# Splitting the wide products of stick-breaking attention, moving the small products of a head, and shifting two operands by 128 bytes

## The chip, the cores and the metric

The kernel runs on one core of one Trainium2 chip. The metric is the device time of one execution in microseconds (us). TensorE (PE) multiplies; VectorE (DVE) and ScalarE (ACT) prepare its operands and take its results away; SyncE (SP) issues the weight transfers; GpSimd (POOL) only fills constants.

## What is computed

A two-layer trunk over 272 positions (16 learned ones ahead of 256 given) of width 2048, in float32. Layer 0 is a Mamba-2 mixer and a gated feed-forward net. From its result one key and one value projection is made. Layer 1 is stick-breaking attention with its own query projection, and a second gated net. The part that the change touches, per head of width 128 and 16 heads:

```
q = (u @ w_q) ; z = q k^T * 128**-0.5
before = kpos < qpos
log_keep = where(before, log_sigmoid(-z), 0)
tail = reverse_cumsum(log_keep) - log_keep
att  = where(before, exp(log_sigmoid(z) + tail), 0)
o    = att @ v ; out = o @ w_o
```

## The kernel before

**A projection** (`project`, lines 140 to 174) makes one tile of 128 output columns for all positions. Its weights come in two halves of 8 blocks of 128 by 128. ACT rounds a half to the type fp32r (line 128, tile `hi`), DVE takes the rest (line 129, tile `lo`), and `mac` makes three matmuls for each block: high weights by low activations (line 142), high by high (143), low by high (144). So a tile is 16 blocks by 3 = 48 matmuls, 272 columns wide where all positions are needed (activations `u0`, `u1`, `y`, `hid`, `ukv`) and 256 wide for the 256 given positions (`uq` for queries, `ob` for the output projection, `u2` for the last gate and up products). There are five `hi` and four `lo` buffers, so ACT and DVE may work that far ahead of PE. `project_block` works on four tiles at a time, half by half, and calls `pump` after each half, which lets waiting side work go on.

**Attention.** The loop over 16 heads m makes the key tile (272 wide), the value tile (272) and the query tile (256); between value and query `others(m)` lets three older heads go on by one stage each. `attend` is a generator with three stages. Stage 1 (head m-1): the scores `psc`, in plain fp32, for queries 0 to 127 against 144 keys (line 685) and queries 128 to 255 against 272 keys (line 686); then mask, two sigmoids, a scan. Stage 2 (head m-2): PE transposes of values (`pt`, line 706) and weights (`pb`, line 710), copied to `vb` and `ab`. Stage 3 (head m-3): `po`, values by weights, in plain fp32, 256 wide (line 725) and 128 wide (line 726). A plain fp32 matmul shows as two records each of line 685, 686, 725 and 726; a transpose shows as one. Every fourth head has two more transposes (lines 713, 714) and a further product (line 728). "Small products" is what follows for this cluster. For the last head the value tile comes after the query, and the last stages of the last heads run between halves of the output projection's first block.

**The last feed-forward net** uses `u2`, and for its down projection a scheme with fewer products, all of whose matmuls are 256 wide and come from line 886 (`three`): stationary tile `sa`, moving tiles `hi`, `lo` and `lq`.

**Addresses.** SBUF tiles are laid out by the pools in the order written. All buffers of `hi` and `lo` start 96 bytes past a multiple of 256, and their blocks are 512 bytes apart. `pair` puts `pad` float32 elements ahead of an activation tile. In the program before, `uq`, `ob` and `u2` start 32 bytes past a multiple of 256, that is, 192 bytes past a multiple of 256 from their weights. `sa` starts at 96, so the moving `hi` and `lo` of line 886 also stand at 192 from it, and `lq` too. `beat` (lines 147 to 150) and `short` put a few 128-wide matmuls with no use for the result ahead of some streams.

Of the kernel before, what the change touches and what calls it, by code (L numbers as in the profile page):

```python
# [6 lines left out]
F32 = mybir.dt.float32  # L7
F32R = mybir.dt.float32r
AF = mybir.ActivationFunctionType
ALU = mybir.AluOpType  # L10
# [3 lines left out]
P = 128  # L14
D = 2048
KD = D // P
SEQ = 256
META = 16
T = SEQ + META
# [8 lines left out]
CONV = 4  # L28
# [5 lines left out]
OQ = 128  # L34
# [6 lines left out]
PAD = {"u": 0, "uq": 64, "y": 0, "ob": 0, "hid": 0, "sa": 16}  # L41
# [16 lines left out]
def trunk(tc, a, out):  # L58
    nc = tc.nc
    V, S, PE = nc.vector, nc.scalar, nc.tensor  # L60
    pin = tc.keep_in_program_order

    with tc.tile_pool(name="const", bufs=1) as cp, \
# [7 lines left out]
        upool = uctx.enter_context(tc.tile_pool(name="up", bufs=1, side="right"))  # L71
# [4 lines left out]

        for k, c in list(PIECES)[:2]:
            nc.scalar.dma_start(h[:, k:k + c, :], a["hT"][:, k:k + c, :])
        cw = upool.tile([P, CONV + 1, 48], F32, name="cw")
        gd = upool.tile([P, 2, 32], F32, name="gd")  # L80
        hd = upool.tile([NH, 2], F32, name="hd")

# [9 lines left out]
        nc.gpsimd.memset(ident, 0.0)  # L92
        nc.gpsimd.affine_select(out=ident, in_=ident, compare_op=ALU.not_equal, fill=1.0,
                                base=0, pattern=[[-1, P]], channel_multiplier=1)
        causal = upool.tile([P, T - OQ], F32, name="causal")
        nc.gpsimd.memset(causal, 1.0)
        nc.gpsimd.affine_select(out=causal, in_=causal, compare_op=ALU.is_ge, fill=0.0,
                                base=0, pattern=[[1, T - OQ]], channel_multiplier=-1)
        sel = upool.tile([P, P], F32, name="sel")
        nc.gpsimd.memset(sel, 1.0)  # L100
        nc.gpsimd.affine_select(out=sel, in_=sel, compare_op=ALU.is_ge, fill=0.0,
                                base=-(P - 1), pattern=[[0, P]], channel_multiplier=1)
# [3 lines left out]
        def nm(s):  # L106
            uid[0] += 1
            return f"{s}_{uid[0]}"
# [25 lines left out]
        def pair(pool, K, n, pad, step, tail=0, **kw):  # L134
            t = pool.tile([P, pad + 2 * K * step + tail], F32R, **kw)
            t = t[:, pad:pad + 2 * K * step].rearrange("p (s k t) -> p s k t", s=2, t=step)
            return [t[:, i, :, :n] for i in range(2)]
# [46 lines left out]
        def times(dst, ps, r):  # L184
            V.tensor_tensor(out=dst, in0=ps[:, :r.shape[-1]], in1=r, op=ALU.mult)
# [48 lines left out]
        u = pair(upool, KD, T, PAD["u"], TP, 24, tag="u", name="u0")  # L234
# [48 lines left out]
        with tc.tile_pool(name="ssd0", bufs=1) as q0, \  # L283
# [25 lines left out]
            with tc.tile_pool(name="dtp", bufs=1) as dq:  # L309

                psd = ptp.tile([P, 512], F32, tag="pt", name=nm("pt"))[:, :T]
                last = piece_w(*PIECES[-1])
                parts = [load(a["w_dt"], k0, LC, NH)[:, :, :NH] for k0 in range(0, KD, LC)]
                for i, w in enumerate(parts):
                    V.tensor_tensor(out=w, in0=w, op=ALU.mult,
                                    in1=gam[:, 0, i * LC:(i + 1) * LC].unsqueeze(2).to_broadcast([P, LC, NH]))
                for j in range(LC):
                    for i, w in enumerate(parts):
                        pin(PE.matmul(psd[i * NH:(i + 1) * NH], w[:, j, :], h[:, i * LC + j, :],  # L319
                                      start=j == 0, stop=j == LC - 1))  # L320
# [10 lines left out]
                v = dq.tile([NH, T], F32, name="v")  # L331
# [37 lines left out]
                pt = ptp.tile([P, 512], F32, tag="pt", name=nm("pt"))  # L369
# [221 lines left out]
            u = pair(upool, KD, T, PAD["u"], TP, 24, tag="u", name="u1")  # L591
# [46 lines left out]
        vpool = vctx.enter_context(tc.tile_pool(name="vp", bufs=1))  # L638
        with tc.tile_pool(name="att1", bufs=1) as b1p, \
                tc.tile_pool(name="att2", bufs=2) as b2p, \  # L640
                tc.tile_pool(name="psa", bufs=3, space=PSUM) as pap:
            uq = pair(vpool, KD, SEQ, PAD["uq"], SEQ, tag="v", name="uq")
            for k in range(KD):
                split_scaled(uq, k, h[:, k, META:], gam[:, 1, k:k + 1])
            ob = pair(b1p, KD, SEQ, PAD["ob"], SEQ, name="ob")
            L0, L1 = META + 128, T
            W = L0 + L1
# [28 lines left out]
            def flat(t):  # L676
                return t.rearrange("p h b k -> p (h b k)")

            def attend(m, kT, qT, vT, vs, ss, pk):
                i = m % SET
                S.copy(vs[:, i], vT.rearrange("p (b k) -> p b k", k=P)[:, 1:, :META])
                psc = pap.tile([P, 512], F32, tag="at", name=nm("psc"))
                PE.matmul(psc[:, :L0], qT[:, 0:128], kT[:, :L0], start=True, stop=True)  # L685
                PE.matmul(psc[:, L0:W], qT[:, 128:256], kT, start=True, stop=True)  # L686
                sc = b2p.tile([P, 2, T], F32, tag="sc", name=nm("sc"))
                ends = sc[:, :, P:L0]
                sc = sc.rearrange("p b k -> p (b k)")[:, :W]
                V.tensor_tensor(out=sc, in0=psc[:, :W], in1=mask, op=ALU.add)  # L690
                kp = b2p.tile([P, W], F32, tag="kp", name=nm("kp"))
                S.activation(kp, sc, AF.Sigmoid, scale=-SCALE)
                S.activation(sc, sc, AF.Sigmoid, scale=SCALE)

                tl = b2p.tile([P, 2, T], F32, tag="tl", name=nm("tl"), bufs=1)
                tails = tl[:, :, P:L0 - 1]
                tl = tl.rearrange("p b k -> p (b k)")
                n = W - 1
                V.tensor_tensor_scan(tl[:, n - 1::-1], kp[:, n:0:-1], reset[:, n - 1::-1],
                                     1.0, ALU.mult, ALU.max)  # L700
                V.tensor_tensor(out=ss[:, i, :, :META - 1], in0=ends[:, :, :META - 1], in1=tails, op=ALU.mult)
                V.tensor_tensor(out=sc[:, :n], in0=sc[:, :n], in1=tl[:, :n], op=ALU.mult)
                yield
                pt = prp.tile([P, 512], F32, tag="pr", name=nm("pt"))
                for b in range(2):
                    pin(PE.transpose(pt[:, b * P:(b + 1) * P], vT[:, b * P:(b + 1) * P], ident))
                vb = b2p.tile([P, 2 * P], F32, tag="vb", name=nm("vb"))
                pb = pap.tile([P, 512], F32, tag="at", name=nm("pb"))
                for b, c in enumerate((0, L0, L0 + P)):
                    pin(PE.transpose(pb[:, b * P:(b + 1) * P], sc[:, c:c + P], ident))  # L710
                ab = b2p.tile([P, 3 * P], F32, tag="ab", name=nm("ab"))
                if i == SET - 1:
                    pin(PE.transpose(pt[:, 256:384], flat(vs), ident))
                    pin(PE.transpose(pt[:, 384:512], flat(ss), ident))
                S.copy(ab, pb[:, :384])
                S.copy(vb, pt[:, :256])
                if i == SET - 1:
                    vsT = b1p.tile([P, P], F32, tag="vsT", name=nm("vsT"))
                    S.copy(vsT, pt[:, 256:384])
                    bd = b1p.tile([P, 2 * SET, META], F32, tag="bd", name=nm("bd"))  # L720
                    V.tensor_tensor(out=bd, in0=pt[:, 384 + E0:512].unsqueeze(1).to_broadcast([P, 2 * SET, META]),
                                    in1=own, op=ALU.mult)
                yield
                po = pap.tile([P, 512], F32, tag="at", name=nm("po"))
                PE.matmul(po[:, :SEQ], vb[:, :P], ab[:, 0:SEQ], start=True, stop=False)  # L725
                PE.matmul(po[:, P:SEQ], vb[:, P:], ab[:, SEQ:], start=False, stop=True)
                if i == SET - 1:
                    PE.matmul(po[:, SEQ:SEQ + P], vsT, bd.rearrange("p g q -> p (g q)"), start=True, stop=True)
                S.copy(ob[0][:, m, :], po[:, :SEQ])
                V.tensor_copy(pk[:, i], po[:, :SEQ].rearrange("p (b k) -> p b k", b=2)[:, :, E0:])  # L730
                V.tensor_tensor(out=ob[1][:, m, :], in0=po[:, :SEQ], in1=ob[0][:, m, :].bitcast(F32),
                                op=ALU.subtract)
                if i == SET - 1:
                    V.tensor_tensor(out=flat(pk), in0=flat(pk), in1=po[:, SEQ:SEQ + P], op=ALU.add)
                    oh, ol = [o[:, m - i:m + 1, :].rearrange("p h (b k) -> p h b k", b=2)[:, :, :, E0:] for o in ob]
                    S.copy(oh, pk)
                    V.tensor_tensor(out=ol, in0=pk, in1=oh.bitcast(F32), op=ALU.subtract)
# [4 lines left out]
            def key(m):  # L742
                kT = b2p.tile([P, T], F32, tag="kT", name=nm("kT"))
                times(kT, pre.pop(0) if pre else project(a["w_kv"][m], ukv), rB)
                return kT
# [13 lines left out]
            def others(m):  # L759
                for k in (m - 3, m - 1, m - 2):  # L760
                    if 0 <= k < len(heads):
                        next(heads[k], None)

            for m in range(KD):
                if m % SET == 0:
                    sets = [shared("vs"), sss[m // SET % 2], shared("pk")]
                kT = key(m)
                if m < KD - 1:
                    vT = value(m)
                others(m)  # L770
                qT = query(m)
                if m == KD - 1:
                    vT = value(m)
                heads.append(attend(m, kT, qT, vT, *sets))
# [8 lines left out]

            side.append(rest())

            u = pair(vpool, KD, SEQ, PAD["uq"], SEQ, tag="v", name="u2")

            def finish_o(m, ps):
                hm = h[:, m, META:]
# [10 lines left out]
        with tc.tile_pool(name="ffn1", bufs=1) as fp, \  # L800
# [215 lines left out]
            for m in range(KF):  # L1016
# [6 lines left out]
                if m % 2 == 0:  # L1023
# [4 lines left out]
                                in1=gt.rearrange("p (b t) -> p b t", b=2), op=ALU.mult)  # L1028
# [48 lines left out]
            for f in (f1, f1, f1, f0, f1, f0, f1, f0):  # L1077
                x = next(f)
# [5 lines left out]
            x = next(f0)  # L1084
# [124 lines left out]
```

## Time and profile before

| what | value |
|---|---|
| median of three runs | 2610.78 us (2610.65 to 2611.01) |
| profiled execution | 2610.9 us, span of its instructions 2608.8 us |
| PE, weight loads, DVE, ACT busy | 2599.6, 2590.4, 1824.0, 1365.8 us |
| matmuls of lines 142 to 144 on `uq` and on `ob` | 768 each |
| matmuls of line 886 with moving `hi` or `lo` | 1674 |
| granted TensorE clock | 0.999 |
| attention's small products | 1531 to 1821 us |
| output projection | 1810 to 1900 us |

Matmuls overlap each other, so a matmul's own duration (say 276 ns) is longer than the time from its start to the start of the next. The latter is what adds up to the span, and is read from start times in the timeline.

### The profile page before, as it was taken

Reading aid. Unit: us, or ns where it says so; the run is one execution under the profiler, and the core shown is the slowest. Engines: PE = TensorE matmul, PEld = TensorE weight load, DVE = VectorE, ACT = ScalarE, POOL = GpSimd, SP = SyncE. Lnnn points to the kernel's source line nnn. Section 1 sums busy time; section 2 is a strip of 40 time slices with the busy share of each in tenths; the row PEclk is TensorE's granted clock in tenths of the full one; section 3 lists DMA queues with packets and bytes.
Section 4 is the critical chain, followed back from the end, with each engine's and each line's share of the span. In section 5 each row is a group of like instructions: output and inputs, shape, how many; then the busy total and the mean of one; then the engine's idle time right before and its main releaser. Section 6 shows DMA issues by size and latency. Waiting matters only on the chain.

```text
span 2608.8 us, 52060 instructions
## 1 busy us (share of the span) xinstructions
PE 2599.6 (100%) x21735; PEld 2590.4 (99%) x21735; DVE 1824.0 (70%) x2713; ACT 1365.8 (52%) x1884; POOL 6.2 (0%) x26
## 2 busy tenths in 40 slices
PE   9999999999999999999999999999999999999998
PEld 9999999999999999999999999999999999999998
DVE  8888767768755554445555565556666888989998
ACT  6766657556544443334444454444554555555554
POOL 0000000000000000000000000000000000000000
PEclk9999999999999999999999999999999999999999
DMA  7666556555555555555555555555655656566665
GB/s 254 202 185 188 185 172 189 178 184 178 173 176 179 179 179 179 180 177 179 179 179 168 183 179 168 158 167 154 194 179 189 205 189 211 194 203 202 208 204 170
DMA packets 159596, 482.46 MB, mean 185 GB/s; under 512 B 21824, under 2 KB 43264, under 8 KB 159360
## 3 DMA queue, kind: packets, MB, share of 16 engines
q1 hardware_dynamic: 159072, 478.86, 58.7%
q8 instruction: 170, 2.79, 0.4%
q14 instruction: 66, 0.54, 0.1%
q10 hardware_dynamic: 288, 0.28, 0.0%
HBM read 476.91 MB, written 2.17 MB: 184 GB/s over the span
## 4 chain that ended last, share of the span: by engine, by line
PE 100%; DVE 0%; ACT 0%; issue 0%; DVEq 0%
PE pp L144 29%; PE pp L142 29%; PE pp L143 29%; PE x L886 7%; PE pp L886 1%; PE py L536 1%; PE py L542 0%; PE pt L449 0%; PE psc L686 0%; PE po L725 0%; PE pb L710 0%; PE pt L319 0%; PE wake L238 0%; PE psc L685 0%; PE pe L143 0%; PE pe L142 0%
## 5 line engine op out<-in xcount | busy, mean ns | idle before, releaser
L128 ACT CAST hi<-raw 128x1024 fp32r<-128x1024 f32 (+1 forms) x802 | 833.2, 1041 | 912.4 <-PE pp L143 747.3
L129 DVE TENSOR_TENSOR lo<-raw,hi 128x1024 fp32r<-128x1024 f32 (+1 forms) x802 | 964.9, 1206 | 282.7 <-issue 149.9
L142 PE MATMUL pp<-u,hi 128*128 128x272 f32 (+1 forms) x4064 | 1147.7, 282 | 0.0
L143 PE MATMUL pp<-u,hi 128*128 128x272 f32 (+1 forms) x4064 | 1145.9, 282 | 0.0
L144 PE MATMUL pp<-u,lo 128*128 128x272 f32 (+1 forms) x4064 | 1145.4, 282 | 0.2 <-DVE lo L129 0.2
L143 PEld LDWEIGHTS pp<-u,hi 128*128 128x128 f32 x4064 | 763.1, 188 | 0.5 <-issue 0.4
L142 PEld LDWEIGHTS pp<-u,hi 128*128 128x128 f32 x4064 | 762.9, 188 | 0.3
L144 PEld LDWEIGHTS pp<-u,lo 128*128 128x128 f32 x4064 | 762.6, 188 | 0.6 <-DVE lo L129 0.6
L142 PE MATMUL pp<-hid,hi 128*128 128x272 f32 x704 | 201.7, 287 | 0.0
L144 PE MATMUL pp<-hid,lo 128*128 128x272 f32 x704 | 201.7, 287 | 0.0
L143 PE MATMUL pp<-hid,hi 128*128 128x272 f32 x704 | 201.7, 286 | 0.0
L886 PE MATMUL x<-hi,sa 128*128 128x256 f32 x1062 | 184.3, 276 | 0.0
L886 PEld LDWEIGHTS x<-hi,sa 128*128 128x128 f32 x1062 | 159.9, 188 | 0.0
L142 PE MATMUL pp<-y,hi 128*128 128x272 f32 x512 | 147.3, 288 | 0.0
L144 PE MATMUL pp<-y,lo 128*128 128x272 f32 x512 | 146.7, 287 | 0.0
L143 PE MATMUL pp<-y,hi 128*128 128x272 f32 x512 | 146.7, 286 | 0.0
L142 PE MATMUL pp<-ukv,hi 128*128 128x272 f32 x512 | 146.3, 286 | 0.0
L143 PE MATMUL pp<-ukv,hi 128*128 128x272 f32 x512 | 146.0, 285 | 0.0
L144 PE MATMUL pp<-ukv,lo 128*128 128x272 f32 x512 | 146.0, 285 | 0.0
L878 ACT CAST hi<-tt 128x1024 fp32r<-128x1024 f32 x73 | 76.9, 1053 | 122.2 <-PE pp L143 61.7
L144 PEld LDWEIGHTS pp<-hid,lo 128*128 128x128 f32 x704 | 132.6, 188 | 0.0
L142 PEld LDWEIGHTS pp<-hid,hi 128*128 128x128 f32 x704 | 132.6, 188 | 0.0
(286 smaller groups left out, 3562.3 us busy)
## 6 DMA issues: line engine op xcount, KB each, us to landing
raw<-w_gu SPq DMA_DIRECT2D x352, 512.0 KB, 3.6
raw<-w_in SPq DMA_DIRECT2D x152, 512.0 KB, 3.6
raw<-w_dn SPq DMA_DIRECT2D x88, 512.0 KB, 4.0
raw<-w_down SPq DMA_DIRECT2D x80, 512.0 KB, 3.4
raw<-w_out SPq DMA_DIRECT2D x64, 512.0 KB, 3.7
raw<-w_kv SPq DMA_DIRECT2D x64, 512.0 KB, 3.5
raw<-w_q SPq DMA_DIRECT2D x32, 512.0 KB, 3.5
raw<-w_o SPq DMA_DIRECT2D x32, 512.0 KB, 3.5
```

Source lines behind the costliest of these rows:

```text
L128: S.copy(hi[:, :n, :m], raw[:, :n, :m])
L129: V.tensor_tensor(out=lo[:, :n, :m], in0=raw[:, :n, :m], in1=hi[:, :n, :m].bitcast(F32), op=ALU.subtract)
L142: PE.matmul(ps[:, :n], wh, xl, start=first, stop=False)
L143: PE.matmul(ps[:, :n], wh, xh, start=False, stop=False)
L144: PE.matmul(ps[:, :n], wl, xh, start=False, stop=last)
L536: pin(PE.matmul(py[i * HD:(i + 1) * HD, c0:c1], xd[b][:, 2 * j + i, :], gm[b][:, 2 * j + i, :], start=True, stop=True))
L878: S.copy(hi[:, :n], src[:, :n])
L886: PE.matmul(ps, st[x][:, b], w[y][:, c], start=f, stop=l, skip_group_check=True)
```

## The change

Three parts:

1. The 272-wide score product and the 256-wide value product are made of three fp32r matmuls each, as in `mac`. `cut` rounds an operand on ACT and takes the rest on DVE; this is done for the keys (`ks`, 272 columns), the second half of the queries (`qs`, 128), the first two blocks of weights (`as`, 256) and the first block of values (`vh`, `vl`, 128). The narrow products stay plain fp32. Tiles of the pool `up` that are no longer in use serve as buffers.
2. `others(m)` is called after the key tile instead of after the value tile.
3. `uq` is moved by 32 elements (128 bytes). `u2` gets 32 elements at its end, so that both have one size; it stays where it was, but what is laid out behind it moves by 128 bytes as well.

```
-            uq = pair(vpool, KD, SEQ, PAD["uq"], SEQ, tag="v", name="uq")
+            uq = pair(vpool, KD, SEQ, PAD["uq"] + 32, SEQ, tag="v", name="uq")
...
+            def cut(hi, lo, src):
+                S.copy(hi, src)
+                V.tensor_tensor(out=lo, in0=src, in1=hi.bitcast(F32), op=ALU.subtract)
+            def passes(ps, w, x, last):
+                PE.matmul(ps, w[0], x[1], start=True, stop=False)
+                PE.matmul(ps, w[0], x[0], start=False, stop=False)
+                PE.matmul(ps, w[1], x[0], start=False, stop=last)
...
-                PE.matmul(psc[:, L0:W], qT[:, 128:256], kT, start=True, stop=True)
+                kh, kl = [upool.tile([P, T], F32R, tag=n, name=nm("ks")) for n in ("ga", "rg")]
+                qh, ql = upool.tile([P, 256], F32R, tag="qs", name=nm("qs")).rearrange("p (s q) -> s p q", s=2)
+                cut(kh, kl, kT)
+                cut(qh, ql, qT[:, 128:256])
+                passes(psc[:, L0:W], (qh, ql), (kh, kl), True)
...
-                S.copy(ab, pb[:, :384])
-                S.copy(vb, pt[:, :256])
+                cut(ah, al, pb[:, :256])
+                cut(vh, vl, pt[:, :P])
+                S.copy(ab, pb[:, 256:384])
+                S.copy(vb, pt[:, P:256])
...
-                PE.matmul(po[:, :SEQ], vb[:, :P], ab[:, 0:SEQ], start=True, stop=False)
-                PE.matmul(po[:, P:SEQ], vb[:, P:], ab[:, SEQ:], start=False, stop=True)
+                passes(po[:, :SEQ], (vh, vl), (ah, al), False)
+                PE.matmul(po[:, P:SEQ], vb, ab, start=False, stop=True)
...
                 kT = key(m)
+                others(m)
                 if m < KD - 1:
                     vT = value(m)
-                others(m)
                 qT = query(m)
...
-            u = pair(vpool, KD, SEQ, PAD["uq"], SEQ, tag="v", name="u2")
+            u = pair(vpool, KD, SEQ, PAD["uq"], SEQ, 32, tag="v", name="u2")
```

In the built program `uq` and `ob` now start 160 bytes past a multiple of 256: their weights lie 192 past a multiple of 256 from them, and they 64 from the weights. The stationary `sa` moves from 96 to 224 while the moving `hi` and `lo` of line 886 stay, so these go from 192 to 64 too; `lq` moves along with `sa` and stays at 192, and so does `u2` to its weights.

On PE, before, the loop pass for head 6, which begins at the end of a value tile (`pp` from `ukv`) and ends at the first matmul of a query tile (`pp` from `uq`); `pr`-bank tile `pt`, and `psc`, `pb`, `po` as above:

```order
L144 MATMUL pp_18970<-ukv,lo_19004 128x272
L725 MATMUL po_19032<-ab_18834,vb_18829 128x256 [waits PE_49]
L726 MATMUL po_19032<-ab_18834,vb_18829 128x128
L728 MATMUL po_19032<-bd_18841,vsT_18839 128x128
L685 MATMUL psc_19043<-kT_18681,qT_18843 128x144 [waits PE_49]
L686 MATMUL psc_19043<-kT_18681,qT_18843 128x272
L706 MATMUL pt_19055<-ident,vT_18525 128x128 [waits PE_49]
L706 MATMUL pt_19055<-ident,vT_18525 128x128
L710 MATMUL pb_19059<-ident,sc_18817 128x128 x3
L142 MATMUL pp_19067<-uq,hi_19070 128x256 [waits Activation_49]
```

On PE, now, the same pass, from the end of the key tile to the first matmul of the value tile:

```order
L144 MATMUL pp_18986<-ukv,lo_19020 128x272
L686 MATMUL po_19048<-as_18846,vh_18839 128x256 [waits PE_49]
L687 MATMUL po_19048<-as_18846,vh_18839 128x256
L688 MATMUL po_19048<-as_18846,vl_18840 128x256
L744 MATMUL po_19048<-ab_18845,vb_18838 128x128
L746 MATMUL po_19048<-bd_18857,vsT_18855 128x128
L694 MATMUL psc_19061<-kT_18742,qT_18922 128x144 [waits DVE_49]
L686 MATMUL psc_19061<-ks_19064,qs_19065 128x272 [waits Activation_49]
L687 MATMUL psc_19061<-ks_19063,qs_19065 128x272
L688 MATMUL psc_19061<-ks_19063,qs_19065 128x272 [waits DVE_49]
L725 MATMUL pb_19088<-ident,sc_18826 128x128 x3
L142 MATMUL pp_19101<-ukv,hi_19104 128x272
```

The two plain products became three matmuls each, the score product now waits for the cut operands, and the whole cluster stands ahead of a 272-wide stream instead of the 256-wide query stream.

On DVE, before, between two `lo` halves around that cluster:

```order
L129 TENSOR_TENSOR lo_19164<-raw_19161,hi_19163 128x1024 [waits DMAHW6_49,DVE_49,Activation_49]
L730 COPY pk_17758<-po_19032 128x32 [waits Activation_49]
L731 TENSOR_TENSOR ob<-po_19032,ob 128x256
L734 TENSOR_TENSOR pk_17758<-pk_17758,po_19032 128x128 [waits DVE_49]
L690 TENSOR_TENSOR sc_19046<-psc_19043,mask 128x416 [waits PE_49]
L737 TENSOR_TENSOR ob<-pk_17758,ob 128x8x16 [waits Activation_49]
L699 SCALAR_TENSOR_TENSOR tl_19051<-kp_19048,reset 128x415 [waits Activation_49]
L701 TENSOR_TENSOR ss_17627<-sc_19046,tl_19051 128x2x15 [waits DVE_49,Activation_49]
L702 TENSOR_TENSOR sc_19046<-sc_19046,tl_19051 128x415 [waits DVE_49]
L129 TENSOR_TENSOR lo_19197<-raw_19194,hi_19196 128x1024 [waits DMAHW7_49,PE_49]
```

On DVE, now, the same place:

```order
L129 TENSOR_TENSOR lo_19198<-raw_19195,hi_19197 128x1024 [waits DMAHW4_49,Activation_49]
L748 COPY pk_17758<-po_19048 128x32 [waits Activation_49]
L749 TENSOR_TENSOR ob<-po_19048,ob 128x256
L752 TENSOR_TENSOR pk_17758<-pk_17758,po_19048 128x128 [waits DVE_49]
L703 TENSOR_TENSOR sc_19073<-psc_19061,mask 128x416 [waits PE_49]
L755 TENSOR_TENSOR ob<-pk_17758,ob 128x8x16 [waits Activation_49]
L683 TENSOR_TENSOR as_19093<-pb_19088,as_19093 128x256 [waits PE_49]
L683 TENSOR_TENSOR vl_19087<-pt_19082,vh_19086 128x128
L712 SCALAR_TENSOR_TENSOR tl_19078<-kp_19075,reset 128x415 [waits Activation_49]
L683 TENSOR_TENSOR ks_19301<-kT_18985,ks_19300 128x272
L714 TENSOR_TENSOR ss_17627<-sc_19073,tl_19078 128x2x15 [waits DVE_49,Activation_49]
L715 TENSOR_TENSOR sc_19073<-sc_19073,tl_19078 128x415 [waits DVE_49]
```

Three of the four subtractions of `cut` stand inside this cluster, ahead of the next `lo` half; the fourth (`qs`) comes two rows after the query tile is taken from PSUM.

More of the change, by code (lines that the diff above doesn't have):

```diff
@@ L78, in trunk @@
             nc.scalar.dma_start(h[:, k:k + c, :], a["hT"][:, k:k + c, :])
-        cw = upool.tile([P, CONV + 1, 48], F32, name="cw")
+        cw = upool.tile([P, 256], F32, tag="qs", name="cw")[:, :(CONV + 1) * 48].rearrange("p (c m) -> p c m", m=48)
         gd = upool.tile([P, 2, 32], F32, name="gd")
@@ L94, in trunk @@
                                 base=0, pattern=[[-1, P]], channel_multiplier=1)
-        causal = upool.tile([P, T - OQ], F32, name="causal")
+        causal = upool.tile([P, T - OQ], F32, tag="vl", name="causal")
         nc.gpsimd.memset(causal, 1.0)
@@ L98, in trunk @@
                                 base=0, pattern=[[1, T - OQ]], channel_multiplier=-1)
-        sel = upool.tile([P, P], F32, name="sel")
+        sel = upool.tile([P, P], F32, tag="vh", name="sel")
         nc.gpsimd.memset(sel, 1.0)
@@ L706, in attend @@
                     pin(PE.transpose(pt[:, b * P:(b + 1) * P], vT[:, b * P:(b + 1) * P], ident))
-                vb = b2p.tile([P, 2 * P], F32, tag="vb", name=nm("vb"))
+                vb = b2p.tile([P, P], F32, tag="vb", name=nm("vb"))
+                vh = upool.tile([P, P], F32R, tag="vh", name=nm("vh"))
+                vl = upool.tile([P, T - OQ], F32R, tag="vl", name=nm("vl"))[:, :P]
                 pb = pap.tile([P, 512], F32, tag="at", name=nm("pb"))
@@ L710, in attend @@
                     pin(PE.transpose(pb[:, b * P:(b + 1) * P], sc[:, c:c + P], ident))
-                ab = b2p.tile([P, 3 * P], F32, tag="ab", name=nm("ab"))
+                ab = b2p.tile([P, P], F32, tag="ab", name=nm("ab"))
+                ah, al = b1p.tile([P, 512], F32R, tag="as", name=nm("as")).rearrange("p (s q) -> s p q", s=2)
                 if i == SET - 1:
```

## The prediction

> **What bounds the kernel.** I read the page first, then the groups by line, then the timeline of PE around the small products, then the groups again in narrow stretches, then the waits of DVE and ACT.
>
> ```profile
> PE 2599.6 (100%) x21735; PEld 2590.4 (99%) x21735; DVE 1824.0 (70%) x2713; ACT 1365.8 (52%) x1884; POOL 6.2 (0%) x26
> PE 100%; DVE 0%; ACT 0%; issue 0%; DVEq 0%
> ```
>
> PE never rests, and the chain that ended last is PE from one end to the other. So the change is worth what it does to the sum of start-to-start times of matmuls, unless it makes PE wait. I cost it on PE alone and then look for new waits.
>
> The timeline of PE for head 4 (start, duration of the merged rows):
>
> ```profile
> 1587.07 0.59 PE L725 MATMUL po<-ab,vb 128*128 128x256 f32 x2
> 1587.50 0.38 PE L726 MATMUL po<-ab,vb 128*128 128x128 f32 x2
> ...
> 1587.97 0.62 PE L686 MATMUL psc<-kT,qT 128*128 128x272 f32 x2
> 1588.43 0.38 PE L706 MATMUL pt<-ident,vT 128*128 128x128 f32 x2
> 1588.64 0.49 PE L710 MATMUL pb<-ident,sc 128*128 128x128 f32 x3
> 1588.89 0.36 PE L142 MATMUL pp<-uq,hi 128*128 128x256 f32 x1
> 1589.09 0.28 PE L143 MATMUL pp<-uq,hi 128*128 128x256 f32 x1
> ...
> 1594.63 0.29 PE L142 MATMUL pp<-ukv,hi 128*128 128x272 f32 x1
> ```
>
> The plain 256-wide product holds PE for 1587.50 - 1587.07 = 0.43 us, the 272-wide one for 1588.43 - 1587.97 = 0.46 us. Then comes a query tile of 48 matmuls; its last 47 start within 1594.63 - 1589.09 = 5.54 us, 117.9 ns each. The query tile of the next head:
>
> ```profile
> 1608.72 0.28 PE L143 MATMUL pp<-uq,hi 128*128 128x256 f32 x1
> ...
> 1614.07 0.29 PE L142 MATMUL pp<-ukv,hi 128*128 128x272 f32 x1
> ```
>
> It takes 5.35 us for the same 47, 113.8 each. Same instructions, same addresses modulo 256, another pace. The groups of single stretches show two paces, here by line 143's mean duration: a slow query tile (1589.1 to 1594.6), a fast one (1608.8 to 1614.05), the end of the first query tile, which follows a value tile directly (1516.5 to 1519.1), and of the output projection its start (1810 to 1815.3 and 1820.6 to 1835) and the rest, after the `beat` (1835.5 to 1894):
>
> ```profile
> L143 PE MATMUL pp<-uq,hi 128*128 128x256 f32 x16 | 4.5, 281 | 0.0
> ...
> L143 PE MATMUL pp<-uq,hi 128*128 128x256 f32 x16 | 4.4, 277 | 0.0
> ...
> L143 PE MATMUL pp<-uq,hi 128*128 128x256 f32 x9 | 2.5, 276 | 0.0
> ...
> L143 PE MATMUL pp<-ob,hi 128*128 128x256 f32 x15 | 4.2, 281 | 0.0
> L143 PE MATMUL pp<-ob,hi 128*128 128x256 f32 x40 | 11.2, 281 | 0.0
> L143 PE MATMUL pp<-ob,hi 128*128 128x256 f32 x173 | 47.8, 276 | 0.0
> ```
>
> A 281 goes with 117.9 ns from start to start, a 276 with the faster pace, which the last feed-forward net shows at its cleanest, 9 steps in 1.02 us or 113.3 ns:
>
> ```profile
> 1999.76 0.28 PE L142 MATMUL pp<-u,hi 128*128 128x256 f32 x1
> ...
> 2000.78 0.28 PE L142 MATMUL pp<-u,hi 128*128 128x256 f32 x1
> ```
>
> The difference is 4.6 ns a matmul. A stretch keeps its pace until something of another shape comes between. Over the whole run:
>
> ```profile
> L886 PE MATMUL x<-hi,sa 128*128 128x256 f32 x1062 | 184.3, 276 | 0.0
> ...
> L143 PE MATMUL pp<-uq,hi 128*128 128x256 f32 x256 | 71.3, 278 | 0.0
> ...
> L143 PE MATMUL pp<-ob,hi 128*128 128x256 f32 x256 | 70.9, 277 | 0.0
> ```
>
> A mean of 278 lies two fifths of the way from 276 to 281: about 6 of the 16 query tiles are slow. For `ob` 277 says a fifth, the 3 x 15 and 3 x 40 matmuls above. Line 886 runs at the fast pace throughout.
>
> **The change, part by part.** *Three matmuls for one plain one.* What three fp32r matmuls cost at 272 columns I read from a key or value stream, 33 steps in 1603.89 - 1599.83 = 4.06 us, 123.0 ns each:
>
> ```profile
> 1599.83 0.28 PE L142 MATMUL pp<-ukv,hi 128*128 128x272 f32 x1
> ...
> 1603.89 0.29 PE L142 MATMUL pp<-ukv,hi 128*128 128x272 f32 x1
> ```
>
> Scores: 0.46 - 3 x 0.123 = 0.09 us saved per head. Values: 0.43 - 3 x 0.1133 to 0.1179 = 0.08 to 0.09. Against it stands one more change from plain fp32 to fp32r per head. Above, three transposes and the first query matmul took 1589.09 - 1588.64 = 0.45 us, where two transposes took 0.21; 3 x 0.105 + 0.118 is 0.43, so a change costs some 0.01. That leaves 0.16 us x 16 heads = 2.6 us.
>
> The Trainium skill, "TensorE: Matmul & The Clock Gate", section "Back-to-back issue gap", gives N/2.4 + 2.5 ns, by which the new matmuls would take 115.8 and 109.2 ns and the split save (0.46 - 0.35 + 0.43 - 0.33) x 16 = 3.4 us. Neither pace of this trace reaches that (123.0; 113.3 and 117.9), so I keep the rows.
>
> *The cuts.* Per head DVE gets four subtractions and ACT four casts, with two copies made narrower. The nearest rows, for 272 columns on DVE and on ACT, and for 256 and 128 on DVE:
>
> ```profile
> L615 DVE TENSOR_TENSOR hid<-ut,hid 128x272 fp32r<-128x272 f32 x44 | 19.5, 443 | 21.4 <-ACT hid L614 21.4
> ...
> L614 ACT CAST hid<-ut 128x272 fp32r<-128x272 f32 x44 | 18.5, 421 | 43.2 <-DVE ut L613 43.2
> ...
> L731 DVE TENSOR_TENSOR ob<-po,ob 128x256 fp32r<-128x256 f32 x16 | 6.7, 416 | 0.0
> ...
> L864 DVE TENSOR_TENSOR sm<-up 128x128 f32<-128x128 f32 x22 | 6.4, 291 | 0.3
> ```
>
> DVE: 443 + 416 + 2 x 291 = 1441 ns more per head; ACT at most 4 x 421 = 1.7 us. The waits between 1515 and 1835 us (waited for, total us, times, longest) say who has time:
>
> ```profile
> ACT hi L128 <- PE pp L143: 164.7, 98, 2.0
> ...
> DVE vT L185 <- PE pp L144: 25.1, 15, 1.7
> DVE kT L185 <- PE pp L144: 24.8, 15, 1.7
> DVE qT L185 <- PE pp L144: 18.3, 15, 1.4
> ```
>
> ACT waits 164.7/16 = 10.3 us per head for PE to free a `hi` buffer, DVE (25.1 + 24.8 + 18.3)/16 = 4.3 us for PE's results. Both run as far ahead as the buffers let them. So the cuts cost nothing, and that is the work which hides them: the key, value and query streams. Queued behind the cuts on DVE are `lo` halves (line 129), which PE needs; they fall back by 1.1 us in the cluster and catch up within a tile. The new waits of the score product are met early: `ks` is cut after the key tile, `qs` after the query tile, and a key tile of 48 x 0.123 = 5.9 us follows before PE asks. Transfers and their order on SP stay.
>
> The one tight place is the end, where stages 2 and 3 of the last head are one half-tile apart in the output projection. Last copy of stage 2, and first matmul of stage 3:
>
> ```profile
> 1817.89 0.29 ACT L719 COPY vsT<-pt 128x128 f32<-128x128 f32 x1
> ...
> 1820.00 0.59 PE L725 MATMUL po<-ab,vb 128*128 128x256 f32 x2
> ```
>
> That is 1.8 us of slack. The two subtractions (0.42 + 0.29) and some 0.4 on ACT take about 1.1 of it. No wait, from 0 to 0.5 us if the queues line up badly.
>
> *Small products between key and value.* Their count stays. What changes is what follows them: a 272-wide stream, which has run at one pace after key and value tiles alike, and the query tile now follows a value tile directly, as the first one did, at 276. Six tiles of 48 change by 4.6 ns: 1.3 us saved, if the new addresses keep the fast pace; 0 if not.
>
> *The 128 bytes.* `uq` (768 matmuls), `ob` (768) and nearly all of line 886's 1674 with moving `hi` or `lo` go from a distance of 192 to one of 64, some 3140 in all. No 256-wide fp32r matmul of the trace stands at 64, so the price is bounded. Above: all at 117.9. Below: half a plain fp32 record, 0.43/4 = 107.5 ns, the least a 256-wide pass takes anywhere. Nearer is this: a 128-wide matmul followed by other weights.
>
> ```profile
> 1835.01 0.34 PE L150 MATMUL beat<-ob,hi 128*128 128x128 f32 x2
> 1835.18 0.28 PE L150 MATMUL beat<-ob,lo 128*128 128x128 f32 x1
> 1835.30 0.33 PE L142 MATMUL pp<-ob,hi 128*128 128x256 f32 x1
> ```
>
> Half the columns, and still 0.12 us to the next start: at 0.113 the 256-wide stream is about as quick as weights change at all. I take 113.3, no change of the fast pace. For the slow start of `ob` (165 matmuls x 4.6 = 0.76 us) I take half, 0.4 us, since whether the small products still leave it slow is open.
>
> **Sum.** 2.6 + 1.3 + 0.4 = 4.3 us. The profiled execution took 2610.9 us, its span 2608.8; the median of the runs, 2610.78, is 0.1 below. 2610.8 - 4.3 = 2606.5 us, or -0.16%. A measurement of this kernel can tell about 0.2%, 5.2 us, from no change: below 2605.6 it counts as faster, above 2616.0 as slower.
>
> **Rivals.** *The new distance is quicker.* At 107.5 it would give 5.8 x 3140 = 18 us, at 111 ns 7.2 us: 2606.5 - 7.2 = 2599.3. For it: 107.5 is seen with plain fp32. Against: the `beat`. From 113.0 on it decides for faster.
>
> *The new distance is slower everywhere, which puts the time on the other side.* All 3140 at 117.9, of which 288 + 165 were slow already: 2690 x 4.6 = 12.4 us lost, 2.6 won by the split: 2620.6. It becomes slower by over 0.2% once more than 1700 fast matmuls turn slow, so line 886 has to be among them. For it: the pace does change without a change of instructions. Against: at 272 columns distances of 160 (`ukv`) and 192 (`hid`) show one pace:
>
> ```profile
> L143 PE MATMUL pp<-hid,hi 128*128 128x272 f32 x704 | 201.7, 286 | 0.0
> ...
> L143 PE MATMUL pp<-ukv,hi 128*128 128x272 f32 x512 | 146.0, 285 | 0.0
> ```
>
> *It is slower in attention alone.* 1536 - 453 = 1080 x 4.6 = 5.0 lost, 2.6 won: 2613.2. Mixtures lie between 2608 and 2613.
>
> *The distance does nothing.* The pace hangs on what came just before, and no address matters: 2.6 + 1.3 = 3.9 us, 2606.9. The Trainium skill, same page, "Step-by-step: what each phase is for", says that PE reads moving operand and weights through two independent ports and that loading the next weights takes nothing from the running matmul. By that rule this rival holds; the two paces at equal addresses neither show nor exclude it.
>
> **How the numbers follow.** Fast pace kept or the distance without effect (2605.3 to 2608): 0.55. Quicker: 0.16. Slower in attention, wholly or in part (2608 to 2613.5): 0.20. Slower everywhere, or PE waiting for the cuts: 0.09. The range leaves out the last and the far half of the second: 2602 to 2613.5. The likeliest alone has 2605.3 to 2608. Faster by over 0.2%: 0.16 and a tenth of 0.55 make 0.22; slower: 0.09; the same: 0.69.
>
> **What would show it.** The scores' and values' three matmuls at 123 and 113 to 118 ns. Line 143 on `uq` at a mean of 276, not 278; on `ob` 276 or 277; line 886 still 276. A 281 in line 886 would prove the slower rival, anything under 276 there the quicker one. Idle time of PE before lines 686 to 688 would mean that a cut came late, which I hold for excluded outside the last head.

## The result, and the profile after

The changed kernel takes 2637.47 us (median of four runs, 2637.2 to 2637.6), the kernel before 2610.84 (2610.65 to 2611.01): a ratio of 1.0101, 95% interval 1.0089 to 1.0113. It is 26.6 us slower. Forecast were 2606.5 us, with 2602.0 to 2613.5 as the range. The profiled execution of after has a span of 2635.7 us, 26.9 more than before, at the same granted clock, 0.999.

From the page of after, the busy times and the chain that ended last:

```profile
PE 2626.9 (100%) x21767; PEld 2620.8 (99%) x21767; DVE 1841.6 (70%) x2777; ACT 1372.8 (52%) x1948; POOL 6.2 (0%) x26
...
PE 100%; DVE 0%; ACT 0%; issue 0%; DVEq 0%
```

PE still never rests and is still the whole chain. Its busy time grew by 27.3 us, about as much as the span, and only 32 records were added. So nothing waits; the matmuls themselves come at longer intervals. Which ones, the groups of after say (busy time, mean ns of one, idle time before):

```profile
L904 PE MATMUL x<-hi,sa 128*128 128x256 f32 x1062 | 190.7, 279 | 0.0
...
L143 PE MATMUL pp<-uq,hi 128*128 128x256 f32 x256 | 71.6, 280 | 0.0
L143 PE MATMUL pp<-ob,hi 128*128 128x256 f32 x256 | 71.5, 279 | 0.0
```

Line 904 is line 886 of before. It went from 276 to 279, `uq` from 278 to 280, `ob` from 277 to 279. But a group's mean can't show that another group, whose code and addresses were left alone, moved too. The gate and up products on `u2` in the stretch from 1990 to 2540 us, in before:

```profile
L143 PE MATMUL pp<-u,hi 128*128 128x256 f32 x1168 | 322.4, 276 | 0.0
```

and in after:

```profile
L143 PE MATMUL pp<-u,hi 128*128 128x256 f32 x1135 | 318.9, 281 | 0.0
```

In the same 550 us 33 fewer of this line fit, and they show 281.

The timeline of PE in after, small products of one head (now behind a key tile) and the second and the last of the 48 matmuls of the query tile that follows (start, duration):

```profile
1581.62 0.28 PE L686 MATMUL po<-as,vh 128*128 128x256 f32 x1
1581.73 0.28 PE L687 MATMUL po<-as,vh 128*128 128x256 f32 x1
1581.85 0.28 PE L688 MATMUL po<-as,vl 128*128 128x256 f32 x1
1581.97 0.38 PE L744 MATMUL po<-ab,vb 128*128 128x128 f32 x2
1582.19 0.41 PE L694 MATMUL psc<-kT,qT 128*128 128x144 f32 x2
1582.34 0.38 PE L686 MATMUL psc<-ks,qs 128*128 128x272 f32 x1
1582.56 0.29 PE L687 MATMUL psc<-ks,qs 128*128 128x272 f32 x1
1582.69 0.29 PE L688 MATMUL psc<-ks,qs 128*128 128x272 f32 x1
1582.82 0.38 PE L719 MATMUL pt<-ident,vT 128*128 128x128 f32 x2
1583.03 0.49 PE L725 MATMUL pb<-ident,sc 128*128 128x128 f32 x3
...
1589.41 0.28 PE L143 MATMUL pp<-uq,hi 128*128 128x256 f32 x1
...
1594.83 0.28 PE L144 MATMUL pp<-uq,lo 128*128 128x256 f32 x1
```

The split does what it was to do: from the first `po` to the first `pb` 1583.03 - 1581.62 = 1.41 us, where before it took 1588.64 - 1587.07 = 1.57. The query tile, 46 steps in 5.42 us, runs at 117.8 ns, although a 272-wide value tile lies directly ahead of it.

The sums of all start-to-start times on PE, added up from the matmul records of each trace by moving operand (us; the runs of the rows below the first two come in the next section; `u` also holds the first layer's input projection, which is alike in all):

| kernel | products on `u`, gate and up of both layers among them | line 886/904 | value and key (`ukv`) | `uq` | `ob` | small products |
|---|---|---|---|---|---|---|
| before | 1477.98 | 214.78 | 189.85 | 90.10 | 88.12 | 30.61 |
| after | 1494.85 | 222.84 | 191.13 | 90.56 | 90.75 | 28.28 |
| undo_shift | 1478.14 | 214.78 | 191.09 | 87.44 | 87.60 | 28.37 |
| after_sa_back | 1478.33 | 214.78 | 191.14 | 90.55 | 90.75 | 28.28 |
| sa_only | 1494.88 | 222.83 | 189.85 | 90.10 | 88.11 | 30.61 |
| split_only | 1477.95 | 214.79 | 189.98 | 91.25 | 87.60 | 28.27 |
| order_only | 1477.97 | 214.78 | 191.42 | 87.46 | 88.12 | 30.61 |

After less before: +16.9 gate and up, +8.1 line 904, +2.6 `ob`, +0.5 `uq`, +1.3 `ukv`, -2.3 small products. Without rounding that is 27.0 in all, the growth of the span within 0.1. The column of line 886/904 includes the products on `lq`, which stay at 192; their share grew too, from 25.1 to 26.0.

### The profile page after: what moved, and what is told of

Same layout as the page of the kernel before. It is cut to its first block, busy times and chain, and to the rows that moved or that the text cites. A ratio compares the mean times of both kernels' runs of the same rounds, so it can differ in the third digit from the quotient of the medians.

```text
span 2635.7 us, 52246 instructions
## 1 busy us (share of the span) xinstructions
PE 2626.9 (100%) x21767; PEld 2620.8 (99%) x21767; DVE 1841.6 (70%) x2777; ACT 1372.8 (52%) x1948; POOL 6.2 (0%) x26
## 4 chain that ended last, share of the span: by engine, by line
PE 100%; DVE 0%; ACT 0%; issue 0%; DVEq 0%
PE pp L143 29%; PE pp L142 29%; PE pp L144 29%; PE x L904 7%; PE pp L904 1%; PE py L536 1%; PE py L542 0%; PE pt L449 0%; PE pb L725 0%; PE wake L238 0%; PE pt L319 0%; PE psc L694 0%; PE pe L143 0%; PE pe L142 0%; PE pe L144 0%; PE pc L491 0%
## 5 line engine op out<-in xcount | busy, mean ns | idle before, releaser
L904 PE MATMUL x<-hi,sa 128*128 128x256 f32 x1062 | 190.7, 279 | 0.0
```

The source lines that it names most:

```text
L904: PE.matmul(ps, st[x][:, b], w[y][:, c], start=f, stop=l, skip_group_check=True)
```

## The experiments

Three theories went in. *Distance with hand-over* (the expectations say inheritance): at 64 bytes from the weights a 256-wide fp32r matmul takes 117.8 ns; at 192 it may take 113.3 or 117.8 and goes on at the pace that it is handed, so that line 904 at 64 slows the products on `u2` behind it, which stay at 192. *Distance without hand-over*: these are slow for another reason. *History*: the split and the new order leave a slow pace behind, and the 128 bytes have no part in it.

**The bytes undone, and the bytes alone.** `undo_shift` is after with this edit; `shift_only` is before with its reverse and nothing else:

```
-            uq = pair(vpool, KD, SEQ, PAD["uq"] + 32, SEQ, tag="v", name="uq")
+            uq = pair(vpool, KD, SEQ, PAD["uq"], SEQ, tag="v", name="uq")
...
-            u = pair(vpool, KD, SEQ, PAD["uq"], SEQ, 32, tag="v", name="u2")
+            u = pair(vpool, KD, SEQ, PAD["uq"], SEQ, tag="v", name="u2")
```

> The changed kernel with the 128 bytes taken back, so that all 256-wide streams stand at 192 from their weights again; split and order stay. Theory of distance (a 256-wide stream at 64 runs at 117.8 ns; at 192 it keeps the pace it is given): line 143 on the queries at 276, line 904 at 276, the last gate and up products at 276, and 2606 to 2609 us. Rival of history (the split products or their new place leave PE in the slow pace, addresses have no part): 2635 to 2638 us, line 904 at 279 as in the changed kernel.

> The kernel before with the 128 bytes alone: queries, output projection and line 886's hi and lo at 64, plain fp32 products, old order. Distance: 2637 to 2641 us, some 2 us above the changed kernel, since the split's gain is missing. History: 2611 us, as before.

`undo_shift` took 2606.55 us (2606.34 to 2606.76) against 2610.97, ratio 0.9983 (0.9974 to 0.9992); `shift_only` 2640.33, ratio 1.0112 (1.0097 to 1.0128). The bytes alone cost 29.4 us, and without them the rest of the change is 4.4 us faster than before. That ends the history theory. The groups of `undo_shift`:

```profile
L904 PE MATMUL x<-hi,sa 128*128 128x256 f32 x1062 | 184.3, 276 | 0.0
...
L143 PE MATMUL pp<-uq,hi 128*128 128x256 f32 x256 | 70.8, 276 | 0.0
L143 PE MATMUL pp<-ob,hi 128*128 128x256 f32 x256 | 70.7, 276 | 0.0
```

All three are at 276; by their start times 15 of the 16 query tiles have the fast pace. Its query tile in the timeline at the place shown of after:

```profile
1588.39 0.28 PE L143 MATMUL pp<-uq,hi 128*128 128x256 f32 x1
...
1593.61 0.28 PE L144 MATMUL pp<-uq,lo 128*128 128x256 f32 x1
```

46 steps in 5.22 us are 113.5 ns. Same order, same instructions, same neighbours as in after; only the 128 bytes differ.

**Which operand.** `after_sa_back` is after with the stationary tile `sa` moved on by 128 bytes, so that line 904 is at 192 again and `uq` and `ob` stay at 64. `sa_only` is before with the same edit, which there puts line 886's `hi` and `lo` at 64 and leaves `uq`, `ob` and `u2` at 192:

```
-            fp.tile([P, PAD["sa"]], F32, name="shift")
+            fp.tile([P, PAD["sa"] + 32], F32, name="shift")
```

> The changed kernel with 32 more elements ahead of the stationary tile of line 904, which brings that line back to 192; queries and output projection stay at 64. Distance: queries and output projection at 281, line 904 and the last gate and up products back at 276, 2611 to 2614 us. History: 2635 to 2638 us. If the shifted queries alone set the pace for all that follows, also 2635 to 2638.

> The kernel before with 32 more elements ahead of the stationary tile of line 886 alone, so that only this line's hi and lo stand at 64. Distance with inheritance (the last gate and up products, themselves at 192, keep the slow pace that line 886 hands them): 2610.8 + 7.9 for line 886 + 16.7 for gate and up = 2633 to 2637 us. Distance without inheritance: line 886 slow, gate and up products fast, 2617 to 2620 us. History: 2611 us.

`after_sa_back`: 2612.83 us (2612.17 to 2613.5), ratio 1.0007 (0.9998 to 1.0016). `sa_only`: 2635.82 (2635.72 to 2635.88), ratio 1.0095 (1.0081 to 1.0109). So 24.6 us of the loss hang on where `sa` lies, a tile that the diff doesn't name; `uq` and `ob` at 64 cost 2612.83 - 2606.55 = 6.3. The groups of `sa_only` between 1990 and 2540 us:

```profile
L143 PE MATMUL pp<-u,hi 128*128 128x256 f32 x1137 | 319.5, 281 | 0.0
```

and of `after_sa_back`:

```profile
L143 PE MATMUL pp<-u,hi 128*128 128x256 f32 x1169 | 322.7, 276 | 0.0
```

Neither edit touches `u2`, its weights or its distance, and still the products on it turn from 276 to 281 and back with line 904. Where it begins is seen in after's timeline (duration min/median/max, first to last start). The first unit of line 904, 21 matmuls, starts at 1946.83, the second at 1962.97. Up to the second, and behind it:

```profile
L144 PE MATMUL pp<-u,lo x68: 276/276/282, 1929.8 to 1959.8; 128*128 128x256 f32 x68
```

```profile
L143 PE MATMUL pp<-u,hi x63: 281/281/281, 1965.9 to 1987.8; 128*128 128x256 f32 x63
```

From there on to the end of the net hardly anything but 256-wide fp32r matmuls follows, with a unit of line 904 again and again. The hand-over has exceptions. By the start times of after, 68 stretches on `u2` come right behind a unit of line 904, and the unit itself is slow each time. 65 of them, 3720 matmuls, run at 117.8 throughout; three, 168 matmuls, are back at 113.3 after three steps. These three stand behind the units at 1946.83, 2191.05 and 2389.04, the only ones of the 68 that themselves come right after 128-wide matmuls (line 839). So the pace of the matmul just before doesn't settle it alone, and what else does no run tells.

**Other distances.** `undo_shift` with `uq` and `ob` moved in steps of 32 bytes and padded at their ends to keep everything else in place. The three kernels differ in two pads only; for `dist_128_0`:

```
-            uq = pair(vpool, KD, SEQ, PAD["uq"], SEQ, tag="v", name="uq")
+            uq = pair(vpool, KD, SEQ, 48, SEQ, 16, tag="v", name="uq")
...
-            ob = pair(b1p, KD, SEQ, PAD["ob"], SEQ, name="ob")
+            ob = pair(b1p, KD, SEQ, 16, SEQ, 48, name="ob")
```

> The kernel with the split and the new order, all at 192 but queries at 128 and the output projection at 0 from their weights (modulo 256). If only 64 is bad: both 276. If only 192 has the fast pace: both 281 (or 279 to 280 with the first ones). If a distance is quicker than 192, durations under 276. Line 904 and the last gate and up products stay at 276 in each case.

> The same with queries at 160 and the output projection at 224. If a band around 192 is good: both 276. If only 192 is: both 281.

> The same with queries at 96 and the output projection at 32. If a band around 64 is bad: both 281. If only 64 is: both 276.

One run of each gave 2616.75, 2612.96 and 2613.59 us, 10.2, 6.4 and 7.0 above `undo_shift`. Their timelines: second and last matmul of a query tile (46 steps apart), and a merged row of `ob` in the output projection. `dist_128_0`, with `uq` at 128 and `ob` at 0:

```profile
1590.18 0.28 PE L143 MATMUL pp<-uq,hi 128*128 128x256 f32 x1
...
1595.70 0.28 PE L144 MATMUL pp<-uq,lo 128*128 128x256 f32 x1
...
L142 PE MATMUL pp<-ob,hi x84: 283/283/283, 1855.0 to 1884.9; 128*128 128x256 f32 x84
```

`dist_160_224`:

```profile
1589.45 0.28 PE L143 MATMUL pp<-uq,hi 128*128 128x256 f32 x1
...
1594.85 0.28 PE L144 MATMUL pp<-uq,lo 128*128 128x256 f32 x1
...
L142 PE MATMUL pp<-ob,hi x85: 277/281/285, 1855.1 to 1884.9; 128*128 128x256 f32 x85
```

`dist_96_32`:

```profile
1589.84 0.29 PE L143 MATMUL pp<-uq,hi 128*128 128x256 f32 x1
...
1595.36 0.28 PE L144 MATMUL pp<-uq,lo 128*128 128x256 f32 x1
...
L143 PE MATMUL pp<-ob,hi x87: 277/279/282, 1854.9 to 1885.0; 128*128 128x256 f32 x87
```

`undo_shift`, with `ob` at 192:

```profile
L142 PE MATMUL pp<-ob,hi x89: 276/276/276, 1855.0 to 1884.9; 128*128 128x256 f32 x89
```

A merged row of x84 spans 3 x 83 steps, since lines 142, 143 and 144 alternate: 29.9/249 = 0.120 us. The rows round their starts to 0.1 us; the start times themselves give as means:

| distance mod 256 | 0 | 32 | 64 | 96 | 128 | 160 | 192 | 224 |
|---|---|---|---|---|---|---|---|---|
| ns from start to start | 120.0 | 116.7 | 117.8 | 120.0 | 120.0 | 117.4 | 113.3, or 117.8 | 118.3 |

Of the eight, 192 alone has the fast pace. All others lie between 116.7 and 120.0.

One rival stays open: that not the distance counts but each operand's own place. In every fast stream here the moving operand starts 32 and the stationary one 96 bytes past a multiple of 256; this holds for line 886 too, whose moving operands start 192 bytes into the buffers `hi` and `lo`. Every stream that the runs put at another distance had only one of the two moved. `lq` alone moves together with its stationary operand, to 160 and 224, and keeps 192. Between 1990 and 2540 us it shows in before and in after

```profile
L886 PE MATMUL x<-lq,sa 128*128 128x256 f32 x193 | 53.4, 277 | 0.0
...
L904 PE MATMUL x<-lq,sa 128*128 128x256 f32 x180 | 50.5, 281 | 0.0
```

It is slow, but it stands among the slow products on `hi`, so this can be the hand-over as well. What follows says distance; the two places would fit as well.

**Split and order apart.** `split_only` is `undo_shift` with the small products back in their old place; `order_only` is before with them in the new one:

```
                 kT = key(m)
-                others(m)
                 if m < KD - 1:
                     vT = value(m)
+                others(m)
                 qT = query(m)
```

> The three matmuls for one plain one alone: old order, old addresses. By the rows of the kernel before 0.16 us per head, 2.6 us in all, 2608.2 us, and up to 1.3 us either way by the pace of the query tiles behind the cluster: 2607 to 2609.5. Rival: the order carries the whole gain of 4.4 us that was measured with both, and the split none: 2611.

> The new place of the small products alone, with plain fp32 products and all at 192. If the query tile takes over the pace of the value tile ahead of it: all query tiles but the last at 276, 6 x 48 x 4.6 ns = 1.3 us less than before, 2609.6 us. Rival: the place has no part and the split alone gave the gain: 2611.

`split_only`: 2609.14 us (2608.96 to 2609.76), ratio 0.9993 (0.9984 to 1.0002). `order_only`: 2610.06 (2609.64 to 2610.26) against 2611.16, ratio 0.9995 (0.9986 to 1.0004). Neither interval excludes no change; the medians are 2.0 and 1.1 lower, and no run of either reaches up to one of before's. Together they give 4.4, which is more than 3.1. The groups tell why. `split_only`:

```profile
L143 PE MATMUL pp<-uq,hi 128*128 128x256 f32 x256 | 71.8, 280 | 0.0
```

and `order_only`:

```profile
L143 PE MATMUL pp<-uq,hi 128*128 128x256 f32 x256 | 70.8, 277 | 0.0
```

With the split in the old place 14 of the 16 query tiles run at 117.8, in before 7: `uq` costs 91.25 us instead of 90.10. Moving the small products gets `uq` down to 87.4 either way, so it is worth 1.2 more once the split is made.

**A reset.** If the products on `u2` only keep the pace that line 904 hands them, something of another shape between the two should give it back. `sa_beat` is `sa_only` with the kernel's own `beat` (three 128-wide matmuls, result unused) after each of the 68 units of line 886 that products on `u2` follow:

```
-            b = prp.tile([P, 512], F32, tag="pr", name=nm("beat"))
+            b = pp.tile([P, 512], F32, tag="pp", name=nm("beat"))
...
-                if k0 == 0 and then:
-                    then()
+                if k0 == 0 and then and then():
+                    beat(hi, lo, x)
```

> The kernel before with line 886 at 64, as in the run with the shifted stationary tile alone, and now three 128-wide matmuls of the next weights (a beat) ahead of the gate and up products after each unit of line 886, some 70 in all. If gate and up at 192 merely take over the pace that line 886 hands them, and a beat sets it anew: line 886 still at 279 to 281, gate and up products at 276; the beats cost about 0.29 to 0.35 us each, 20 to 24 us, so 2639 to 2642 us less the 16.7 that gate and up gain, and without that gain 2656 to 2660. Rival: gate and up are slow for a reason of their own, and stay at 281: 2656 to 2660 us.

One run: 2644.33 us, 8.5 more than `sa_only`. From 1990 to 2540 us its groups show

```profile
L143 PE MATMUL pp<-u,hi 128*128 128x256 f32 x1117 | 308.4, 276 | 0.0
```

while line 886, over the whole run, stays slow:

```profile
L886 PE MATMUL x<-hi,sa 128*128 128x256 f32 x1062 | 191.4, 280 | 0.0
```

The gate and up products of line 143 went from 281 to 276 with no SBUF address changed (lines 142 and 144 show 279 and 277: they hold the slowest of the first steps behind each beat). This is the hand-over by itself. It doesn't pay: the beats take 19.2 us from start to start and line 886 1.2 more, gate and up win 11.8, not 16.7, since the first few matmuls behind a beat are slow: 19.2 + 1.2 - 11.8 = 8.6. The time is 2.3 above the upper end expected for this theory and 12 below the lower end of the other.

## Why the prediction was wrong

**The 128 bytes: here it failed.** The step took "113.3, no change of the fast pace" for 64, between bounds of 107.5 and 117.9. Measured is 117.8, the upper bound. Put at nothing, the step cost 4.5 us in attention and 8.1 on line 886 (in before's order), and 16.9 on the products on `u2`, which it had no term for: 29.5, against 29.4 for the bytes alone. Two arguments misled it.

- The `beat` was taken to show that 113 ns is about as quick as weights change. That speaks against anything quicker, and nothing quicker was found; it said nothing on whether the pace could be lost.
- The 272-wide streams at 160 and 192 ran alike. The 272-wide pace of about 123 ns was the same at these two, the only distances that the 272-wide projections have here; a shape that shows no effect is no witness for one that does. That before had two paces at one distance made history look like the cause; it was a second cause, and all 256-wide fp32r matmuls of that trace stood at 192, so the first could not show there.

The sign it set for the slower rival, a 281 in line 886, came as 279: at 64 a record of 279 to 280 goes with 117.8 ns from start to start, so the pace is to be read from the starts.

**The rival on the other side was right in kind and too small by more than half.** *Slower everywhere* gave 2620.6, with 0.09 as its chance together with waits. Its terms hold: 12.4 us forecast as lost in attention and line 886; measured are 4.5 for attention (2640.33 - 2635.82, in before's order) and 8.1 for line 886, 12.6 together. That these sums meet is in part luck: 0.9 of the 8.1 lie on `lq`, which stays at 192 and wasn't counted. What it left out are the products on `u2`. Their distance stays, so they weren't counted, though the prediction itself had the rule "A stretch keeps its pace until something of another shape comes between": line 886 and the products on `u2` are both 256 wide, and nothing comes between. The 3720 of these that keep the slow pace make 16.7 at 4.5 ns; measured 16.9. With that term the rival would have read 2637.3. The rule itself is a little too strong: in three of 68 stretches the fast pace came back with nothing between.

*Slower in attention alone* gave 2613.2; the kernel that makes this case, `after_sa_back`, took 2612.83.

*The distance does nothing* falls: the same matmuls with the same neighbours take 113.5 or 117.8 ns by where their operands lie. The Trainium skill says in "TensorE: Matmul & The Clock Gate", section "Step-by-step: what each phase is for", that loading the next weights takes no SBUF read bandwidth from the running matmul. For these streams the conclusion that the prediction drew from it, that no address matters, doesn't hold, and the measurement decides. Whether the loads are the reason no run shows.

**Three matmuls for one plain one: right in the sum, a little too high.** 0.16 us a head and 2.6 in all were forecast. The head shown gives 0.16; over all 16 the small products' sum fell by 2.3 in after, 0.15 a head. The part on the scores came another way than forecast. Their three matmuls take 1582.82 - 1582.34 = 0.48 us, no less than the 0.46 of the plain product, since the first, behind a plain one, takes 0.22 and not 0.123. The gain on the scores lies in the narrow plain product ahead of them, which holds PE for 1582.34 - 1582.19 = 0.15 us and in before held it for 1587.97 - 1587.72 = 0.25:

```profile
1587.72 0.41 PE L685 MATMUL psc<-kT,qT 128*128 128x144 f32 x2
```

The formula that the prediction set beside this, from the Trainium skill's section "Back-to-back issue gap", is given there for isolated matmuls and not for streams in which each has its own weights; so these paces don't speak against it.

**The cuts: right.** Idle time of PE ahead of lines 686 to 688 is nil, in the last head too.

**The order: right once the bytes are gone.** 1.3 plus 0.4 were forecast for `uq` and `ob`. `undo_shift` has -2.7 on `uq`, -0.5 on `ob` and +1.2 on `ukv`, since the slow first step behind the transposes is now a 272-wide one's: -1.9. Six query tiles went fast, as forecast: before has 7 slow ones, and the last, which no value tile precedes, stays slow. With -2.2 on the small products that is -4.2 (rounded sums), and the median is 4.4 lower. So the sum with nothing for the bytes was right, 2606.5 against 2606.55, if closer than its terms: one is 0.4 too high, the other 0.2 too low. That kernel is faster than both; the change as built loses it to 128 bytes.

## What to carry to other kernels

Before a tile is padded or moved, list the distance between moving and stationary operand, and the place of each, modulo 256, for every hot matmul whose tiles lie behind it: here the tile that cost most, `sa`, wasn't named in the diff. Price a slower pace not only for the matmuls whose addresses change but for all of the same shape that follow without a break (here 16.9 of 29.4 us). When all rows of a profile share one value of what is about to change, they bound nothing on its effect; the far bound deserves real weight.

## What was not expected of the hardware

The pace of 256-wide fp32r matmuls, each with new weights, hangs on where the operands lie modulo 256 bytes: 113.3 ns at best at a distance of 192, 116.7 to 120.0 at the seven others tried. At 192 there are two steady paces, 113.3 and 117.8, and a stream mostly keeps what it is handed for tens of microseconds (63 matmuls of each of three kinds at 281 in 22 us, without one that went back; 65 of 68 stretches in all); a few 128-wide matmuls bring it back to the fast one. At 64 they don't: `ob` follows a `beat` in after as well and shows 279. At 272 columns, where the projections stand at 160 and 192 only, neither is seen. Which part of the chip makes it so no run here tells; only the fp32r type and the lengths of this kernel were tried, and distances in steps of 32 bytes.
